# Attention transposes in runs over two PSUM banks held as one tile

## The chip, the cores and the metric

The kernel runs on one core of a Trainium2 chip. The core has five engines that run side by side: TensorE (in the profile PE for its matmuls, PEld for the weight loads ahead of them), VectorE (DVE), ScalarE (ACT), GpSimd (POOL) and SyncE (SP), which issues most DMA transfers. Matmuls write to PSUM, which has eight banks of 128 partitions x 512 fp32 values; DVE and ACT read it from there. The metric is the time of one execution on the device in microseconds (us); lower is better.

## The reference

One residual block over 1040 positions (16 learned meta tokens and 1024 frames), model width 1024, in fp32:

```
xn   = rms_norm(h, g0);  proj = xn @ w_in
o_a  = forgetting_attention(q_a, k_a, v_a, log_f)     # 8 heads of 64: softmax(q k^T/8 + c[t] - c[s]), s <= t
o_b  = stick_breaking_attention(q_b, k_b, v_b)        # 8 heads of 64: sigmoid(z[t,s]) * prod_{s<j<t}(1 - sigmoid(z[t,j]))
mix  = (sigmoid(g_a)*(o_a @ w_o_fox) + sigmoid(g_b)*(o_b @ w_o_sb)) @ w_out
h    = h + rms_norm(mix, g1)
u    = causal_depthwise_conv(rms_norm(h, g2) @ w_up)  # 3 taps
h    = h + rms_norm((gelu(u_gate)*u_val) @ w_down, g3)
```

Only the attention of both kinds, and the projections that run beside it, bear on what follows.

## The kernel before

Every fp32 operand is split into a high and a low part, and a product is made of three matmuls: high x high, high x low, low x high (`products`, L118). Data lie with features on the partitions and positions along the row, in three pieces of 260, 390 and 390 positions (`PCS`).

The attention runs over 16 heads, first eight forgetting ones (b = 0), then eight stick-breaking ones (b = 1). `prep(x + 1)` projects queries and keys of the next head (`qk_head`, tile pq) and, for each second head, the values of a pair of heads (`v_pair`, tile pv), while `attention` works on the present one; after that `gate(x)` projects a block of the gates (tile pg). The last seven gates follow behind the heads.

`attention` takes the queries in four blocks c of 256, two times 128. `weights_of` makes the two tiles of attention weights (pr, with queries on the partitions): scores by matmuls into a bank of psS, then for a forgetting head exponential and normalization, for a stick-breaking head two sigmoids and a product scan along the row on DVE (L403). The weights must then have keys on the partitions, so TensorE transposes them, 128 x 128 at a time, into a bank of psT: first the 16 meta keys (tile tm, L414, two transposes), then for each g up to c a group of up to four (tile tr, L424; three where g = c, since one of the four is above the diagonal). ACT copies the bank to the high part of pt (L428), DVE subtracts that from the bank for the low part (L429), and matmuls of pt with the values add into the one bank of psO (tile po, L418 and L434). Per head that is 8 transposes into tm and 36 into tr. The values need transposes too: eight into two tiles vtr (L300) and one into vtm (L305) for each pair of heads.

The eight banks of PSUM in this part: two for projections (pool pl, tile tag lin); psS, psT and psO share six, 3 + 2 + 1 for forgetting and 2 + 3 + 1 for stick-breaking heads. A tile of a pool can be taken again when everything that reads the one before it in that bank has been done. Each engine runs its instructions in one fixed order. A planner makes that order when the program is built, with a model of the instructions' times; the order of the source is its priority. `after(ins)` lets an instruction be issued on its engine only behind `ins`. The hardware then runs each engine's list in order, and an instruction that waits holds up all behind it on that engine.

At the start the first values (pv) go through psT, and the norm's sums and row (`rstd_row`, L138 to L151, tiles rp and rr) through psS.

Of the kernel before, what the change touches and what calls it, by code (L numbers as in the profile page):

```python
# [8 lines left out]
F32 = mybir.dt.float32  # L9
F32R = mybir.dt.float32r  # L10
AF = mybir.ActivationFunctionType
ALU = mybir.AluOpType
# [4 lines left out]
P = 128  # L17
# [32 lines left out]
def block_kernel(ctx, tc, xa, xb, wqk, wv, wf, bfg, wg, wo, wout, wup, wdn, gains, conv, cst, out):  # L50
    nc = tc.nc

    def f(ap):
        return ap.bitcast(F32)
# [110 lines left out]
    with ExitStack() as pa:  # L165
# [4 lines left out]

        pps = pa.enter_context(ExitStack())

        def psum_pools(ns, nt):
            pps.close()
            return [pps.enter_context(tc.tile_pool(name=n, reuse_waits="tile", bufs=k, space=PSUM))
                    for n, k in (("psS", ns), ("psT", nt), ("psO", 1))]

        psS, psT, psO = psum_pools(3, 2)

        ap1 = pa.enter_context(tc.tile_pool(name="ap1", reuse_waits="tile", bufs=1))  # L180
        ap2 = pa.enter_context(tc.tile_pool(name="ap2", reuse_waits="tile", bufs=2))
# [23 lines left out]
        def x_stats(i):  # L205
            n0, n1 = PCS[i]
            w = n1 - n0
            ss = []
            for k in range(0, KT, 4):
                sq = n1p.tile([P, 4, w], F32, tag="sq", bufs=1, name=f"sq{i}{k}")  # L210
                xk = xrs[i][:, k : k + 4, :]
                if i == 0:
                    nc.scalar.activation(sq, xk, AF.Square)
                else:
                    nc.gpsimd.tensor_tensor(sq, xk, xk, op=ALU.mult)
                ss.append(n1p.tile([P, w], F32, tag="ss", name=f"ss{i}{k}"))
                nc.vector.tensor_reduce(ss[-1], sq.rearrange("p k t -> p t k"), axis=AX.X, op=ALU.add)
            nc.scalar.copy(rs1[:, n0:n1], rstd_row(ss, w, n1p, psS, "s", f"a{i}"))


        def forget():
# [59 lines left out]
        def v_pair(b, p):  # L281
            hi, lo = load_w(wv[b * 4 + p], KT * P, f"v{b}{p}", hv=b or p)
            yield
            vt = ap1.tile([P, L], F32, tag="vt", name=f"vt{b}{p}")
            for i, (n0, n1) in enumerate(PCS):
                if b == 0 and p == 0:
                    ps = psT.tile([P, 512], F32, tag="tr", name=f"pv{b}{p}{i}")
                else:
                    ps = pl.tile([P, 512], F32, tag="lin", name=f"pv{b}{p}{i}")
                products(ps[:, : n1 - n0], hi, lo, xs[i], 0, KT, 0, n1 - n0)  # L290
                with tc.high_priority(offset=200):
                    nc.vector.tensor_tensor(vt[:, n0:n1], ps[:, : n1 - n0], rs1[:, n0:n1], op=ALU.mult)
                yield
            vps, vtag = (psT, "tr") if b else (psS, "s")
            vv = ap2.tile([P, 8, 2, 2, DH], F32R, tag="vv", name=f"vv{b}{p}")
            for g in range(2):
                pt = vps.tile([P, 4, 2, DH], F32, tag=vtag, name=f"vtr{b}{p}{g}")
                for j in range(4):
                    c0 = NM + (4 * g + j) * P
                    nc.tensor.transpose(pt[:, j, :, :].rearrange("p a b -> p (a b)"), vt[:, c0 : c0 + P], ident)  # L300
                hv = vv[:, 4 * g : 4 * g + 4, :, 0, :]
                nc.scalar.copy(hv, pt)
                nc.vector.tensor_tensor(vv[:, 4 * g : 4 * g + 4, :, 1, :], pt, f(hv), op=ALU.subtract)
            pt = vps.tile([P, 4, 2, DH], F32, tag=vtag, name=f"vtm{b}{p}")
            nc.tensor.transpose(pt[0:NM, 0, :, :].rearrange("p a b -> p (a b)"), vt[:, 0:NM], ident)  # L305
            vm = vms[p % 2]
            src = pt[0:NM, 0, :, :]
            nc.scalar.copy(vm[0:NM, :, 0, :], src)
            nc.scalar.copy(vm[32:48, :, 0, :], src)
            nc.vector.tensor_tensor(vm[0:NM, :, 1, :], src, f(vm[0:NM, :, 0, :]), op=ALU.subtract)  # L310
            nc.vector.tensor_tensor(vm[32:48, :, 1, :], src, f(vm[0:NM, :, 0, :]), op=ALU.subtract)
            st = ap2.tile([NM, 2, DH], F32, tag="vst", bufs=1, name=f"vst{b}{p}")
            nc.scalar.copy(st, src)
            for hh in range(2):
                h = 2 * p + hh
                nc.sync.dma_start(vmini[b][NM * h : NM * (h + 1), :], st[:, hh, :])
            yield vv, vm
# [45 lines left out]
        def weights_of(b, h, qk, i):  # L363
# [40 lines left out]
                nc.gpsimd.tensor_tensor(pr[:, : w - 1], pr[:, : w - 1], kp[:, 1:w], op=ALU.mult)  # L404
            return pr

        def attention(b, h, qk, vv, vm):
            p, hh = h // 2, h % 2
            for c in range(4):
                prs = [weights_of(b, h, qk, 2 * c + tb) for tb in range(2)]  # L410
                po = psO.tile([P, 256], F32, tag="o", name=f"po{b}{h}{c}")
                tm = psT.tile([P, 512], F32, tag="tr", name=f"tm{b}{h}{c}")
                for tb in range(2):
                    nc.tensor.transpose(tm[0:NM, tb * P : (tb + 1) * P], prs[tb][:, 0:NM], ident)  # L414
                pm = ptm[c % 2]
                nc.scalar.copy(pm[0:NM, :], tm[0:NM, 0:256])
                nc.vector.tensor_tensor(pm[32:48, :], tm[0:NM, 0:256], f(pm[0:NM, :]), op=ALU.subtract)
                nc.tensor.matmul(po, vm[:, hh, :, :].rearrange("p a b -> p (a b)"), pm, start=True, stop=False)  # L418
                for g in range(c + 1):
                    last = g == c  # L420
                    tl = [(2 * g, 0), (2 * g, 1)] + ([] if last else [(2 * g + 1, 0)]) + [(2 * g + 1, 1)]
                    tr = psT.tile([P, 512], F32, tag="tr", name=f"tr{b}{h}{c}{g}")
                    for x, (j, tb) in enumerate(tl):
                        nc.tensor.transpose(tr[:, x * P : (x + 1) * P],  # L424
                                            prs[tb][:, NM + j * P : NM + (j + 1) * P], ident)
                    n = P * len(tl)
                    pt = apl.tile([P, 2, 512], F32R, tag="pt", bufs=3, name=f"pt{b}{h}{c}{g}")
                    nc.scalar.copy(pt[:, 0, :n], tr[:, :n])  # L428
                    nc.vector.tensor_tensor(pt[:, 1, :n], tr[:, :n], f(pt[:, 0, :n]), op=ALU.subtract)  # L429
                    for j in range(2):  # L430
                        vj = vv[:, 2 * g + j, hh, :, :].rearrange("p a b -> p (a b)")
                        for s in range(2):
                            o0 = P if (last and j == 1) else 0
                            nc.tensor.matmul(po[:, o0:256], vj, pt[:, s, 256 * j : min(256 * j + 256, n)],  # L434
                                             start=False, stop=(last and j == 1 and s == 1))
                ot = apl.tile([DH, 256], F32, tag="ot", name=f"ot{b}{h}{c}")
                nc.scalar.copy(ot, po[DH:P, :])
                os_ = apl.tile([DH, 256], F32, tag="os", name=f"os{b}{h}{c}")
                nc.vector.tensor_tensor(os_, po[0:DH, :], ot, op=ALU.add)
                nc.sync.dma_start(od[b][p][hh * DH : (hh + 1) * DH, 2 + 256 * c : 258 + 256 * c], os_)  # L440
                if c == 0 and h == NH - 1:
                    mini(b)

        def mini(b):
# [12 lines left out]
            else:  # L457
                nc.scalar.activation(w, s, AF.Sigmoid)
                nc.scalar.activation(s, s, AF.Sigmoid, scale=-1.0)
                for h in range(NH):  # L460
                    r = s[:, h, :][:, ::-1]
                    nc.vector.tensor_tensor_scan(r, r, r, 1.0, op0=ALU.mult, op1=ALU.bypass)
                nc.vector.tensor_tensor(w[:, :, 0 : NM - 1], w[:, :, 0 : NM - 1], s[:, :, 1:NM], op=ALU.mult)
            tp = psT.tile([P, 512], F32, tag="tr", name=f"mt{b}")
            nc.tensor.transpose(tp[:, 0:2], w.rearrange("p a b -> p (a b)"), ident[0:2, 0:2])
            e = ap1.tile([P, 2], F32, name=f"me{b}")
            nc.scalar.copy(e, tp[:, 0:2])
            x = ap1.tile([P, NH, 2], F32, name=f"mx{b}")
            nc.vector.tensor_tensor(x, e.unsqueeze(1).to_broadcast([P, NH, 2]),
                                    bmask.unsqueeze(2).to_broadcast([P, NH, 2]), op=ALU.mult)  # L470
            po = psT.tile([P, 512], F32, tag="tr", name=f"mo{b}")
            nc.tensor.matmul(po[0:DH, 0:16], vmini[b], x.rearrange("p a b -> p (a b)"), start=True, stop=True)
            o = ap1.tile([DH, NH, 2], F32, name=f"mos{b}")
            nc.scalar.copy(o, po[0:DH, 0:16].rearrange("p (a b) -> p a b", a=NH))
# [48 lines left out]
        for x, (b, h) in enumerate(heads):  # L523
            qk, (vv, vm) = nxt
            attention(b, h, qk, vv, vm)
            if x + 1 == NH:
                psS, psT, psO = psum_pools(2, 3)
                kpp = side_pool("kpp", 2)
                smask = kpp.tile([P, 2, P], F32R, tag="mask", bufs=1, name="smask")
                raw = apl.tile([P, L], F32, tag="pr", bufs=6, name="smask_raw")[:, :P]  # L530
                nc.sync.dma_start(raw, cst[:, CW + P : CW + 2 * P])
                nc.vector.tensor_copy(smask[:, 0, :], ident)
                nc.vector.tensor_copy(smask[:, 1, :], raw)
            if x + 1 < len(heads):
                nxt = prep(x + 1)
            if x < len(heads) - LATE:
                gate(x)
# [552 lines left out]
```

## Time and profile before

| | |
|---|---|
| median of 3 runs | 1690.51 us (1689.75 to 1694.01) |
| profiled execution | 1691.7 us, span of its instructions 1689.8 us |
| granted TensorE clock, mean | 0.992 of full speed |
| TensorE matmul busy | 1644.3 us, 97% of the span |
| DVE, ACT, POOL busy | 1098.2, 819.9, 450.4 us |
| attention's transposes (tr) | first at 103.3 us, last at 729.9 us |

A row of a group reads: line, engine, operation, tiles written <- read, shape, count | busy time in all, mean duration in ns | idle time of the engine just before, and who ended it. The recorded durations of matmuls overlap: the next one starts well before the end of the one before, so what one costs is read from the distance between starts. A row of the timeline merges neighbouring instructions of one kind: start, length from the first start to the last end, count.

### The profile page before, as it was taken

To read this page: it belongs to the slowest core of one execution; us is meant where nothing else is said; L and a number is where in the kernel's file an instruction comes from. 1 tells how busy PE (TensorE), PEld (TensorE's weight loads), DVE (VectorE), ACT (ScalarE), POOL (GpSimd) and SP (SyncE) were. 2 spreads that over 40 slices of the span, in tenths; PEclk is the share of its full clock that TensorE was granted. 3 is DMA by queue.
4 is the path that set the end of the run, shared out by engine and by line. 5 is a ranking of instruction groups with operands and counts; after the bars stand their busy time and mean duration, and the time that the engine had idled before them with its cause. 6 is when DMAs were issued, how large, how long until landed. Compare 5 with 4: busy or idle time off the path is not lost.

```text
span 1689.8 us, 29746 instructions
## 1 busy us (share of the span) xinstructions
PE 1644.3 (97%) x11656; PEld 1584.0 (94%) x11656; DVE 1098.2 (65%) x1849; ACT 819.9 (49%) x1702; POOL 450.4 (27%) x312
## 2 busy tenths in 40 slices
PE   6999999999999999999999999999999999999997
PEld 6899999999999999999999999999999999787787
DVE  8555656655677776745535887888987867333622
ACT  4334545534566665543434555556555556333321
POOL 3446566655566665412211000000000000000001
PEclk9899999999999999999999999999999999999999
DMA  4122121221211111255343452333322226344741
GB/s 170 54 66 65 50 68 57 59 70 49 64 42 28 45 42 50 68 176 176 120 128 111 144 194 91 99 116 121 107 85 91 93 89 213 123 148 138 239 125 63
DMA packets 78076, 170.59 MB, mean 101 GB/s; under 512 B 10320, under 2 KB 33616, under 8 KB 77936
## 3 DMA queue, kind: packets, MB, share of 16 engines
q1 hardware_dynamic: 77392, 168.16, 31.4%
q8 instruction: 92, 1.51, 0.4%
q10 hardware_dynamic: 544, 0.52, 0.1%
q14 instruction: 48, 0.39, 0.1%
HBM read 126.43 MB, written 35.77 MB: 96 GB/s over the span
## 4 chain that ended last, share of the span: by engine, by line
PE 86%; DVE 5%; DMA 3%; issue 3%; ACT 2%; POOL 0%; SPq 0%; DVEq 0%; ACTq 0%; POOLq 0%
PE A L799 12%; PE pd L928 11%; PE pq L118 10%; PE pg L118 9%; PE B L799 6%; PE pm L622 6%; PE y L118 5%; PE pv L118 4%; PE pu L622 4%; PE po L434 4%; PE tr L424 4%; PE R L799 3%; PE s L352 2%; PE s L353 2%; DMA gr<-gdr 2%
## 5 line engine op out<-in xcount | busy, mean ns | idle before, releaser
L974 POOL TENSOR_TENSOR acc<-acc,hr 128x512 f32<-128x512 f32 x4 | 5.0, 1276 | 737.0 <-DVE acc L967 737.0
L928 PE MATMUL pd<-g,wh_d 128*128 128x512 f32 x616 | 193.3, 394 | 2.9 <-ACT wh_d L106 1.6
L928 PEld LDWEIGHTS pd<-g,wh_d 128*128 128x128 f32 x616 | 115.4, 188 | 30.8 <-ACT wh_d L106 2.8
L729 DVE SCALAR_TENSOR_TENSOR c<-us,cb,c 128x512 f32<-128x512 f32 x176 | 128.6, 745 | 23.1 <-ACT c L727 22.4
L400 POOL TENSOR_SCALAR pr<-pr,mx 128x144 f32<-128x144 f32 (+3 forms) x64 | 114.7, 1797 | 102.9 <-DVE mx L399 67.5
L429 DVE TENSOR_TENSOR pt<-tr,pt 128x512 fp32r<-128x512 f32 (+1 forms) x160 | 98.5, 632 | 49.2 <-ACT pt L428 46.2
L928 PE MATMUL pd<-g,wl_d 128*128 128x512 f32 x308 | 121.2, 394 | 2.0 <-DVE wl_d L92 1.9
L403 DVE TENSOR_TENSOR_SCAN kp<-kp 128x144 f32<-128x144 f32 (+3 forms) x64 | 101.9, 1605 | 23.1 <-ACT kp L385 21.3
L434 PE MATMUL po<-pt,vv 128*128 128x256 f32 (+1 forms) x640 | 110.1, 280 | 1.3 <-DVE pt L429 1.2
L404 POOL TENSOR_TENSOR pr<-pr,kp 128x143 f32<-128x143 f32 (+3 forms) x64 | 82.6, 1300 | 97.8 <-DVE kp L403 61.5
L92 DVE TENSOR_TENSOR wl_d<-wr_d,wh_d 128x896 fp32r<-128x896 f32 (+1 forms) x42 | 47.7, 1136 | 92.4 <-ACT wh_d L106 91.1
L428 ACT CAST pt<-tr 128x512 fp32r<-128x512 f32 (+1 forms) x160 | 83.3, 545 | 42.4 <-PE tr L424 40.6
L393 ACT ACTIVATE pr<-s,mx 128x144 f32<-128x144 f32 (+6 forms) x112 | 59.8, 540 | 76.2 <-DVE mx L391 60.5
L434 PEld LDWEIGHTS po<-pt,vv 128*128 128x128 f32 x640 | 94.5, 189 | 2.2 <-DVE pt L429 1.6
L424 PE MATMUL tr<-cs,pr 128*128 128x128 f32 x576 | 91.5, 274 | 0.0
L106 ACT CAST wh_d<-wr_d 128x896 fp32r<-128x896 f32 (+1 forms) x42 | 41.1, 979 | 97.0 <-PE pd L928 84.3
L352 PE MATMUL s<-k,q 128*128 128x264 f32 (+9 forms) x240 | 80.4, 338 | 0.2
L118 PE MATMUL pq<-xh,wh_qk 128*128 128x390 f32 (+1 forms) x384 | 79.1, 331 | 0.0
L727 ACT ACTIVATE c<-us,cb 128x512 f32<-128x512 f32 x88 | 71.7, 816 | 14.2 <-DMA gdr<-c 9.2
L118 PE MATMUL pq<-xl,wh_qk 128*128 128x390 f32 (+1 forms) x384 | 78.5, 331 | 0.0
L118 PE MATMUL pq<-xh,wl_qk 128*128 128x390 f32 (+1 forms) x384 | 77.8, 328 | 0.0
L118 PE MATMUL pg<-xh,wh_g 128*128 128x390 f32 (+1 forms) x384 | 73.9, 324 | 2.0 <-DVE qkt L333 1.5
(291 smaller groups left out, 4550.8 us busy)
## 6 DMA issues: line engine op xcount, KB each, us to landing
wu<-in_wup SPq DMA_DIRECT2D x40, 512.0 KB, 3.3
wr_d<-in_wdn SPq DMA_DIRECT2D x28, 448.0 KB, 3.6
gdr<-c SPq DMA_DIRECT2D x44, 256.0 KB, 2.5
gr<-gdr SPq DMA_DIRECT2D x44, 256.0 KB, 4.0
gs<-gd SPq DMA_DIRECT2D x16, 513.0 KB, 5.0
wr_qk<-in_wqk SPq DMA_DIRECT2D x16, 512.0 KB, 3.8
wr_g<-in_wg SPq DMA_DIRECT2D x16, 512.0 KB, 3.2
wr_wo<-in_wout SPq DMA_DIRECT2D x16, 512.0 KB, 3.4
```

The costliest lines, as they stand in the source:

```text
L118: marks["mm"] = nc.tensor.matmul(ps, w[:, k * P : (k + 1) * P], x[:, k - k0, n0:n1], start=(k == k0 and s == 0), stop=(k == k1 - 1 and s = ...
L352: nc.tensor.matmul(ps[:tn, :n], q2[:, t0 : t0 + tn], k1[:, s0:s1], start=True, stop=False)
L400: nc.gpsimd.tensor_scalar(pr[:, :w], pr[:, :w], z, None, op0=ALU.mult)
L403: nc.vector.tensor_tensor_scan(r, r, r, 1.0, op0=ALU.mult, op1=ALU.bypass)
L424: nc.tensor.transpose(tr[:, x * P : (x + 1) * P], prs[tb][:, NM + j * P : NM + (j + 1) * P], ident)
L428: nc.scalar.copy(pt[:, 0, :n], tr[:, :n])
L429: nc.vector.tensor_tensor(pt[:, 1, :n], tr[:, :n], f(pt[:, 0, :n]), op=ALU.subtract)
L434: nc.tensor.matmul(po[:, o0:256], vj, pt[:, s, 256 * j : min(256 * j + 256, n)], start=False, stop=(last and j == 1 and s == 1))
L622: nc.tensor.matmul(ps, (hi, hi, lo)[s][:, c : c + P], xs[kh][s == 1][:, k, :], start=(s == 0 and kh == 0 and k == 0), stop=(s == 2 and kh ...
L729: nc.vector.scalar_tensor_tensor(c, u[:, :, tap : tap + 256], cb[:, x, tap : tap + 1], c, op0=ALU.mult, op1=ALU.add)
L799: nc.tensor.matmul(ps, w[:, (k0 + i) * P : (k0 + i + 1) * P], x[:, i, :], start=(first and s == 0 and i == 0), stop=(s == 2 and i == 3), s ...
L928: nc.tensor.matmul(ps, a[:, (k - k0) * P : (k - k0 + 1) * P], x[:, c0:c1], start=(k == 0 and s == 0), stop=(k == NK - 1 and s == 2))
```

## The change

The two (or three) single banks of psT become one tile of two banks (tag tr), taken and given back as a whole; in the stick-breaking heads a third bank (tag one) takes what needs only one. `banks` hands these out. A new function `turned` makes one run: for a block c, the groups of keys are taken as [0] together with the meta keys, then [1, 2], then [3]. All transposes of a run are written first, in reversed order, the one whose input is made last in front, and the rest issued behind it; after that come the copies, subtractions and products of the run's groups. A forgetting head so has 1 + 2 + 2 + 3 = 8 runs. The values' two tiles vtr are one run too, each transpose behind the one in front of it, for forgetting heads now also in psT instead of psS. At the start the first values go to psS instead of psT, and the norm's sums and row to the one bank of psO instead of psS. Counted over the program, 137 places remain at which TensorE changes from a transpose to a product, instead of 214.

```diff
-        def psum_pools(ns, nt):
+        def psum_pools(ns):
             pps.close()
             return [pps.enter_context(tc.tile_pool(name=n, reuse_waits="tile", bufs=k, space=PSUM))
-                    for n, k in (("psS", ns), ("psT", nt), ("psO", 1))]
+                    for n, k in (("psS", ns), ("psT", 1), ("psO", 1))]
-        psS, psT, psO = psum_pools(3, 2)
+        psS, psT, psO = psum_pools(3)
+        def banks(b, n, name):
+            if n == 1 and b:
+                return [psT.tile([P, 512], F32, tag="one", name=name)]
+            two = psT.tile([P, 2, 512], F32, tag="tr", name=name)
+            return [two[:, i, :] for i in range(n)]
...
-            nc.scalar.copy(rs1[:, n0:n1], rstd_row(ss, w, n1p, psS, "s", f"a{i}"))
+            nc.scalar.copy(rs1[:, n0:n1], rstd_row(ss, w, n1p, psO, "o", f"a{i}"))
...
-                    ps = psT.tile([P, 512], F32, tag="tr", name=f"pv{b}{p}{i}")
+                    ps = psS.tile([P, 512], F32, tag="s", name=f"pv{b}{p}{i}")
...
-            vps, vtag = (psT, "tr") if b else (psS, "s")
-            for g in range(2):
-                pt = vps.tile([P, 4, 2, DH], F32, tag=vtag, name=f"vtr{b}{p}{g}")
+            lead = None
+            vts = [t.rearrange("p (j a b) -> p j a b", j=4, a=2) for t in banks(b, 2, f"vtr{b}{p}")]
+            for g, pt in enumerate(vts):
                 for j in range(4):
                     c0 = NM + (4 * g + j) * P
-                    nc.tensor.transpose(pt[:, j, :, :].rearrange("p a b -> p (a b)"), vt[:, c0 : c0 + P], ident)
+                    with after(lead):
+                        lead = nc.tensor.transpose(pt[:, j, :, :].rearrange("p a b -> p (a b)"), vt[:, c0 : c0 + P], ident)
+            for g, pt in enumerate(vts):
                 hv = vv[:, 4 * g : 4 * g + 4, :, 0, :]
...
+        def turned(b, h, c, gs, prs, po, vv, vm):
+            hh = h % 2
+            jobs = []
+            free = banks(b, len(gs) + (gs[0] == 0), f"tr{b}{h}{c}{gs[0]}")
+            if gs[0] == 0:
+                tm = free.pop(0)
+                jobs.append((tm, [(tm[0:NM, tb * P : (tb + 1) * P], prs[tb][:, 0:NM]) for tb in (1, 0)]))
+            tls = {}
+            for g in gs:
+                last = g == c
+                tls[g] = [(2 * g, 0), (2 * g, 1)] + ([] if last else [(2 * g + 1, 0)]) + [(2 * g + 1, 1)]
+                tr = free.pop(0)
+                jobs.append((tr, [(tr[:, x * P : (x + 1) * P], prs[tb][:, NM + j * P : NM + (j + 1) * P])
+                                  for x, (j, tb) in reversed(list(enumerate(tls[g])))]))
+            lead = None
+            for _, turns in reversed(jobs):
+                for dst, src in turns:
+                    with after(lead):
+                        t = nc.tensor.transpose(dst, src, ident)
+                    lead = lead or t
...
+            for g, (tr, turns) in zip(gs, jobs):
+                pt = apl.tile([P, 2, 512], F32R, tag="pt", bufs=3, name=f"pt{b}{h}{c}{g}")
+                nc.scalar.copy(pt[:, 0, :n], tr[:, :n])
+                nc.vector.tensor_tensor(pt[:, 1, :n], tr[:, :n], f(pt[:, 0, :n]), op=ALU.subtract)
...
+                for gs in [[0]] + [list(range(g, min(g + 2, c + 1))) for g in range(1, c + 1, 2)]:
+                    turned(b, h, c, gs, prs, po, vv, vm)
```

More of the change, by code (lines that the diff above doesn't have):

```diff
@@ L303, in v_pair @@
                 nc.vector.tensor_tensor(vv[:, 4 * g : 4 * g + 4, :, 1, :], pt, f(hv), op=ALU.subtract)
-            pt = vps.tile([P, 4, 2, DH], F32, tag=vtag, name=f"vtm{b}{p}")
+            pt = banks(b, 1, f"vtm{b}{p}")[0].rearrange("p (j a b) -> p j a b", j=4, a=2)
             nc.tensor.transpose(pt[0:NM, 0, :, :].rearrange("p a b -> p (a b)"), vt[:, 0:NM], ident)
@@ L405, in weights_of @@
             return pr
+        def turned(b, h, c, gs, prs, po, vv, vm):
[18 more added lines that the diff above has]
+                    lead = lead or t
+            if gs[0] == 0:
+                tm = jobs.pop(0)[0]
+                pm = ptm[c % 2]
+                nc.scalar.copy(pm[0:NM, :], tm[0:NM, 0:256])
+                nc.vector.tensor_tensor(pm[32:48, :], tm[0:NM, 0:256], f(pm[0:NM, :]), op=ALU.subtract)
+                nc.tensor.matmul(po, vm[:, hh, :, :].rearrange("p a b -> p (a b)"), pm, start=True, stop=False)
+            for g, (tr, turns) in zip(gs, jobs):
+                last = g == c
+                n = P * len(turns)
+                pt = apl.tile([P, 2, 512], F32R, tag="pt", bufs=3, name=f"pt{b}{h}{c}{g}")
+                nc.scalar.copy(pt[:, 0, :n], tr[:, :n])
+                nc.vector.tensor_tensor(pt[:, 1, :n], tr[:, :n], f(pt[:, 0, :n]), op=ALU.subtract)
+                for j in range(2):
+                    vj = vv[:, 2 * g + j, hh, :, :].rearrange("p a b -> p (a b)")
+                    for s in range(2):
+                        o0 = P if (last and j == 1) else 0
+                        nc.tensor.matmul(po[:, o0:256], vj, pt[:, s, 256 * j : min(256 * j + 256, n)],
+                                         start=False, stop=(last and j == 1 and s == 1))
         def attention(b, h, qk, vv, vm):
@@ L411, in attention @@
                 po = psO.tile([P, 256], F32, tag="o", name=f"po{b}{h}{c}")
[L412 to L435, printed above, removed]
+                for gs in [[0]] + [list(range(g, min(g + 2, c + 1))) for g in range(1, c + 1, 2)]:
+                    turned(b, h, c, gs, prs, po, vv, vm)
                 ot = apl.tile([DH, 256], F32, tag="ot", name=f"ot{b}{h}{c}")
@@ L463, in mini @@
                 nc.vector.tensor_tensor(w[:, :, 0 : NM - 1], w[:, :, 0 : NM - 1], s[:, :, 1:NM], op=ALU.mult)
-            tp = psT.tile([P, 512], F32, tag="tr", name=f"mt{b}")
+            tp = banks(b, 1, f"mt{b}")[0]
             nc.tensor.transpose(tp[:, 0:2], w.rearrange("p a b -> p (a b)"), ident[0:2, 0:2])
@@ L470, in mini @@
                                     bmask.unsqueeze(2).to_broadcast([P, NH, 2]), op=ALU.mult)
-            po = psT.tile([P, 512], F32, tag="tr", name=f"mo{b}")
+            po = banks(b, 1, f"mo{b}")[0]
             nc.tensor.matmul(po[0:DH, 0:16], vmini[b], x.rearrange("p a b -> p (a b)"), start=True, stop=True)
@@ L526, in block_kernel @@
             if x + 1 == NH:
-                psS, psT, psO = psum_pools(2, 3)
+                psS, psT, psO = psum_pools(2)
                 kpp = side_pool("kpp", 2)
```

## The prediction

> **What bounds the kernel now.** I read the page first, then the windows by stage, then the groups of TensorE, then single stretches of the timeline.
>
> ```profile
> PE 1644.3 (97%) x11656; PEld 1584.0 (94%) x11656; DVE 1098.2 (65%) x1849; ACT 819.9 (49%) x1702; POOL 450.4 (27%) x312
> ...
> PE 86%; DVE 5%; DMA 3%; issue 3%; ACT 2%; POOL 0%; SPq 0%; DVEq 0%; ACTq 0%; POOLq 0%
> ```
>
> TensorE is busy for 97% of the span, and 86% of the chain that ended last lies on it. A change to the transposes can therefore pay only in two ways: less TensorE time per instruction, or less waiting. The windows show how much waiting there is.
>
> ```profile
> 17.00:60.00 43.00, 39.25 (x205) 37.64 (x205) 33.89 (x33) 8.64 (x18) 20.80 (x10) 0.80 0.24 88
> ...
> 103.00:390.00 287.00, 287.00 (x2000) 284.13 (x1999) 174.34 (x469) 137.46 (x384) 174.24 (x110) 1.00 0.21 61
> ...
> 420.00:735.00 315.00, 307.69 (x2182) 301.84 (x2182) 225.57 (x310) 183.48 (x469) 177.72 (x123) 0.99 0.17 49
> ```
>
> The columns are length, then busy time of PE, PEld, DVE, ACT and POOL, then granted clock. In the forgetting heads (103 to 390 us) PE is never idle: nothing can be gained from a wait there, only lost. In the stick-breaking heads (420 to 735 us) it is idle for 315.0 - 307.7 = 7.3 us. At the start (17 to 60 us) it is idle for 3.8 us and its clock is 0.80. Behind 735 us the change touches nothing.
>
> **Instructions.** The change neither adds nor removes an instruction on an engine; it moves them.
>
> ```profile
> L424 PE MATMUL tr<-cs,pr 128*128 128x128 f32 x576 | 91.5, 274 | 0.0
> ...
> L414 PE MATMUL tm<-cs,pr 128*16 128x128 f32 x128 | 28.9, 272 | 0.0
> ...
> L300 PE MATMUL vtr<-cs,vt 128*128 128x128 f32 x64 | 9.7, 275 | 0.7 <-DVE vt L292 0.7
> ...
> L305 PE MATMUL vtm<-cs,vt 128*16 128x128 f32 x8 | 2.2, 272 | 0.0
> ```
>
> That is 576 + 128 + 64 + 8 = 776 transposes before and after, and the same products. The last column matters: the attention's transposes, 704 of them, have never held PE up (0.0 us of idle time before them).
>
> **What a change from transpose to product costs.** The words of the change count 214 such places before and 137 after, 77 fewer. Their price can be read where short runs of transposes stand among equal products:
>
> ```profile
> 403.50 0.49 PE L424 MATMUL tr<-cs,pr 128*128 128x128 f32 x3
> 403.75 0.49 PE L118 MATMUL pq<-xl,wh_qk 128*128 128x260 f32 x2
> 404.08 0.51 PE L434 MATMUL po<-pt,vv 128*128 128x256 f32 x3
> 404.43 0.38 PE L414 MATMUL tm<-cs,pr 128*16 128x128 f32 x2
> 404.56 0.48 PE L118 MATMUL pq<-xl,wh_qk 128*128 128x260 f32 x2
> 404.88 1.12 PE L118 MATMUL pq<-xh,wl_qk 128*128 128x260 f32 x8
> 405.84 0.34 PE L118 MATMUL pq<-xh,wh_qk 128*128 128x390 f32 x1
> ```
>
> Eight undisturbed products take 405.84 - 404.88 = 0.96 us, 0.12 each. The two products behind a run of transposes take 0.33 us (403.75 to 404.08) and 0.32 us (404.56 to 404.88) where 0.24 would do: each change seems to cost some 0.08 us. But the run ahead of them is short by as much. Inside a run one transpose takes (0.49 - 0.27) / 2 = 0.11 us, its recorded duration being 0.27; three of them would be 0.33 us, and the product starts after 0.25; two would be 0.22, and it starts after 0.13. So the last transpose of a run occupies PE for about 0.03 us and the product behind it for 0.08 more, and the two add up to what a transpose inside a run costs. Over both places: 3 transposes and 2 products took 0.58 us against 0.33 + 0.24 = 0.57; 2 and 2 took 0.45 against 0.46. The price of a change is 0.00 us, give or take 0.01. I take 3 ns: 77 x 3 ns = **0.2 us gained**. The upper bound, if only the 0.08 us behind the run counted, is 77 x 0.083 = 6.4 us; it speaks against it that the first row is short by the same time, so I take the near end.
>
> **What the two-bank tile costs.** Before, each of two banks (three in the stick-breaking heads) comes free by itself. Afterwards the next run waits until both banks are read: transposes, copy by ACT, subtraction by DVE, and the second bank's subtraction behind the first one's. This pair of tiles shows the time:
>
> ```profile
> 306.67 0.60 PE L424 MATMUL tr<-cs,pr 128*128 128x128 f32 x4
> 307.03 0.40 PE L352 MATMUL s<-k,q 128*128 128x328 f32 x1
> ...
> 311.21 0.64 PE L434 MATMUL po<-pt,vv 128*128 128x256 f32 x4
> 311.68 0.60 PE L424 MATMUL tr<-cs,pr 128*128 128x128 f32 x4
> ```
>
> ```profile
> 307.24 0.68 DVE L429 TENSOR_TENSOR pt<-tr,pt 128x512 fp32r<-128x512 f32 x1
> 307.84 0.83 DVE L383 TENSOR_REDUCE mx<-s 128x1 f32<-128x264 f32 x2
> 308.58 0.68 DVE L429 TENSOR_TENSOR pt<-tr,pt 128x512 fp32r<-128x512 f32 x1
> ```
>
> ```profile
> L428 ACT CAST pt<-tr x160: 452/578/644, 105.4 to 730.2; 128x512 fp32r<-128x512 f32 x96, 128x384 fp32r<-128x384 f32 x64
> L429 DVE TENSOR_TENSOR pt<-tr,pt x160: 526/679/693, 106.1 to 730.7; 128x512 fp32r<-128x512 f32 x96, 128x384 fp32r<-128x384 f32 x64
> L424 PE MATMUL tr<-cs,pr x576: 270/272/301, 103.3 to 729.9; 128*128 128x128 f32 x192
> ```
>
> From the last start of a run: 0.27 + 0.58 + 0.68 + 0.68 = 2.2 us until both banks are read, and the pair above did it in 309.26 - 307.03 = 2.2 us. The room for it: 16 heads in 729.9 - 103.3 us are 39.2 us each. A forgetting head has eight runs (one, two, two and three for its four blocks of queries) and, per pair of heads, two for the values, nine in all: one every 4.35 us. Here PE had 311.68 - 307.03 = 4.65 us of other work between two transposes. A full run of eight is 8 x 0.11 = 0.9 us; 0.9 + 2.2 = 3.1 us of 4.35. On average the wait is hidden by the products that stand between the runs, and I cost it at **nothing in the forgetting heads**. If this cover is gone, it costs up to 2.2 us a run: the transpose that waits holds up everything behind it on PE (pq, pg, po, scores), and DVE's drains of those wait in turn.
>
> In the stick-breaking heads the same subtractions queue behind the scans:
>
> ```profile
> L403 DVE TENSOR_TENSOR_SCAN kp<-kp 128x912 f32<-128x912 f32 x8 | 21.6, 2701 | 2.6 <-ACT kp L385 2.6
> L403 DVE TENSOR_TENSOR_SCAN kp<-kp 128x1040 f32<-128x1040 f32 x8 | 20.1, 2514 | 6.3 <-ACT kp L385 5.3 <-POOL kb L92 1.0
> ...
> L403 DVE TENSOR_TENSOR_SCAN kp<-kp 128x784 f32<-128x784 f32 x8 | 14.3, 1786 | 0.4 <-ACT kp L385 0.3
> ```
>
> There single-bank runs have a bank of their own, so the pair is taken six times a head, but I keep the tighter 4.35 us, since runs are not evenly spread. A scan of up to 4.35 - 2.2 = 2.1 us in front of a subtraction stays hidden; the 784 wide ones do, the 912 and 1040 wide ones exceed it by 0.6 and 0.4 us. If each of these 16 met an evacuation: 8 x 0.6 + 8 x 0.4 = 8 us; if none, 0. I take a third, since scans are 101.9 us of these 315, **2.7 us lost**.
>
> **The other edits.** At the start the sums of the norm move to the one bank of the output pool, the first values from the two transposed banks to the three score banks.
>
> ```profile
> 35.65 1.69 PE L118 MATMUL pv<-xh,wh_v 128*128 128x390 f32 x8 [1.45 <-DVE vt L292]
> ...
> 38.91 1.72 PE L138 MATMUL rp_a<-cs,ss 128*128 128x1 f32 x14 [0.85 <-DVE ss L217]
> ...
> 51.39 2.95 PE L138 MATMUL rp_a<-cs,ss 128*128 128x1 f32 x14 [1.45 <-DVE ss L217]
> ```
>
> The 1.45 us at 35.65 may go, as a third bank is free; but the sums behind wait for DVE anyway, at 38.91 and again at 51.39, and DVE would be late next. One bank for the sums costs nothing for the same reason: each set waits for DVE's reduction, not for a bank. I take 0; the ends are -1.45 us and, from the clock of 0.80 over 43 us (8.6 us lost, which another pattern of waits could halve or raise by half), about 4 us either way. The first transpose of a run is now the one whose input is ready last; those that ran ahead of it before leave early by less, which moves no work. No DMA is added, and none is moved past another in program order.
>
> **Sum.** Profiled execution 1691.7 us (span 1689.8 and 1.9 around it) - 0.2 + 0 + 2.7 + 0 = 1694.2. It lies 1.2 us above the median of 1690.51 shown, so a median of **1693 us**.
>
> **Rivals.**
> *B, the pair's wait shows: slower.* In 4 places of each forgetting head and 2 of each stick-breaking one, a run follows another of the same block of queries, with its input long there: 8 x 4 + 8 x 2 = 48 places. The tile alone decides when it may start. If the written order keeps there only the 8 products of the run in front (8 x 0.12 = 1 us), 2.2 - 1.0 = 1.2 us is lost each time; it decides as soon as less than 2.2 us of other work stands between two runs. All 48 would be 58 us; I price one in four, 12 x 1.2 = 14 us: 1705 us. For it: banks go from two or three that turn to one pair, and the forgetting heads have no idle time to absorb anything. Against it: 4.65 us stood between above. The Trainium skill's Perfetto Trace Analysis (Optimizing Tensor Performance, Matmuls) speaks against this change: independent groups should rotate through different banks, so that the evacuation of one lies under the matmuls of the next. No row of before shows a transpose that lacked a bank, so it is not yet borne out here.
> *C, faster.* Either the 0.08 us behind a run is real after all, -6.4 us, or the re-planned order loses most of the 7.3 us of idle time in the stick-breaking heads: 1684 us either way. Against the first stand the rows at 403.50 and 404.43; for the second, that all instructions there are placed anew; against it:
>
> ```profile
> PE pv L118 <- DVE qkt L333: 3.2, 2, 1.9
> ```
>
> these waits are for drains behind scans, which the change leaves alone.
> *D, it doesn't do what it says.* Each transpose is tied only to the first of its run, so products could still be placed inside: 1691 us.
>
> **Chances.** A (1693, own range 1688 to 1698) 0.39; B 0.33; C 0.25; D 0.03. About 0.3%, 5 us, is what can be told from no change. A: 0.31 same, 0.03 faster, 0.05 slower; B: 0.30 slower, 0.03 same; C: 0.22 faster, 0.03 same; D same. Faster 0.25, same 0.40, slower 0.35. The range reaches down over C with the clock's 4 us, to 1680, and up over B to one and a half times its price, to 1713.
>
> **What would show it.** Right: the same 776 transposes at 0.11 us inside a run, products behind a run still 0.08 us late, idle time before the transposes under 3 us, PE full from 103 to 390 us. B: idle time before transposes, released by DVE's subtraction. C: the sum of transpose and product falling below its parts, or the stick-breaking window idle for under 2 us. What I take on trust is that the order keeps work between the runs; a changed clock at the start would also make me wrong.

## The result

The changed kernel takes 1835.3 us (median of 4 runs, 1832.7 to 1837.7) where the kernel before takes 1690.2 us: ratio 1.085, 95% interval 1.083 to 1.088. It is slower by 145 us, far outside the range of 1680 to 1713 us.

The page of the changed kernel, parts 1 and 4, with the granted clock of part 2:

```profile
PE 1712.7 (93%) x11656; PEld 1623.2 (88%) x11656; DVE 1104.2 (60%) x1849; ACT 828.6 (45%) x1702; POOL 446.1 (24%) x312
...
PEclk9999898989989989999699999999999999999998
...
PE 76%; DVE 9%; ACT 5%; DMA 4%; issue 4%; POOL 1%; SPq 0%; DVEq 0%; ACTq 0%; POOLq 0%
```

The instructions are the same in number (11656 matmuls), but TensorE's share of the chain fell from 86 to 76%, DVE's and ACT's rose, and the clock is below full in slices where it was full before.

For the stages, cut at the first transpose of the first head, that of the ninth head (the first stick-breaking one) and the first product of the output projections (tile y), here are the windows of the kernel before, and then of the changed one. Columns: length, busy PE, PEld, DVE, ACT, POOL, clock, share and rate of the DMA.

```profile
103.20:456.50 353.30, 352.30 (x2443) 348.34 (x2441) 215.03 (x560) 169.34 (x468) 208.19 (x135) 1.00 0.20 60
456.50:751.10 294.60, 288.30 (x2044) 283.10 (x2043) 210.65 (x289) 172.02 (x435) 160.96 (x109) 0.99 0.20 56
```

```profile
103.70:523.80 420.10, 391.31 (x2443) 371.60 (x2442) 216.92 (x558) 172.51 (x469) 206.38 (x136) 0.93 0.17 50
523.80:885.70 361.90, 319.71 (x2084) 302.05 (x2082) 210.52 (x278) 171.34 (x420) 156.51 (x108) 0.95 0.16 46
885.70:998.50 112.80, 99.78 (x769) 97.73 (x770) 60.00 (x133) 48.02 (x86) 25.16 (x31) 0.92 0.47 142
```

The forgetting heads lost 66.8 us, the stick-breaking heads 67.3; of the difference of the spans, 146.1 us, 12 are left for all else, most of it the first products of y. Of the 66.8 us, idle time of PE is 28.8 - 1.0 = 27.8; the other 39.0 us are in PE's busy time, which grew with the same 2443 matmuls. The clock of 0.93 accounts for some 0.07 x 420 = 29 us of that.

The loss is not spread over the heads. For the first pair of heads:

```profile
103.70:179.60 75.90, 75.75 (x518) 74.97 (x517) 41.92 (x118) 34.07 (x96) 47.60 (x31) 1.00 0.23 69
179.60:209.00 29.40, 22.64 (x96) 18.91 (x96) 13.77 (x39) 11.00 (x29) 8.52 (x6) 0.71 0.02 5
```

For 76 us PE is full at full clock; then come 29 us with 96 matmuls, 6.8 us of idle time and a clock of 0.71. The other three pairs go the same way: PE almost full for 74 to 75 us, then 29.3, 28.9 and 33.4 us at a clock of 0.77, 0.76 and 0.74. Nearly all idle time of these heads, and every fall of the clock, lies in these four dry stretches at the end of each pair.

What PE waited for in the changed kernel, the longest first in total:

```profile
PE po L453 <- DVE pt L448: 15.9, 27, 1.6
PE rp_a L138 <- DVE ss L224: 14.5, 3, 10.9
PE y L118 <- DVE t L616: 11.9, 1, 11.9
PE po L442 <- DVE ptm L441: 9.8, 9, 1.7
PE s L361 <- ACT pr L395: 6.6, 11, 1.9
PE po L453 <- ACT pt L447: 6.0, 13, 0.7
...
PE vtm L314 <- DVE mx L400: 4.4, 2, 2.3
...
PE vtm L314 <- DVE vv L312: 2.4, 1, 2.4
...
PE tr L435 <- POOL pr L413: 1.3, 1, 1.3
```

The attention's transposes (tr) still wait for almost nothing, 1.3 us. Most of the wait stands before the products po of a run, for the copy and the subtraction of their own run: 15.9 + 9.8 + 6.0 = 31.7 us, 12.4 of them in the forgetting heads. There the values' meta transposes (vtm) wait another 4.4 + 2.4 = 6.8 us, behind the reading of the values' pair of banks. When a transposed group has not yet been read, nothing else is left in PE's order to do.

Two stretches show how that comes. First a filled one, at the start of the heads: the runs on PE, and on DVE the subtraction that ends each run's hold of the pair (the time from its first transpose until both banks have been read).

```profile
103.66 0.71 PE L435 MATMUL tr<-cs,pr 128*128 128x128 f32 x5
...
111.08 0.82 PE L435 MATMUL tr<-cs,pr 128*128 128x128 f32 x6
...
118.50 0.49 PE L435 MATMUL tr<-cs,pr 128*128 128x128 f32 x3
...
122.77 0.81 PE L435 MATMUL tr<-cs,pr 128*128 128x128 f32 x6
```

```profile
106.09 0.56 DVE L448 TENSOR_TENSOR pt<-tr,pt 128x384 fp32r<-128x384 f32 x1 [0.55 <-ACT pt L447]
...
114.02 0.68 DVE L448 TENSOR_TENSOR pt<-tr,pt 128x512 fp32r<-128x512 f32 x1
...
119.54 0.56 DVE L448 TENSOR_TENSOR pt<-tr,pt 128x384 fp32r<-128x384 f32 x1 [1.78 <-ACT pt L447]
```

The pair was free at 106.65, 114.70 and 120.10 us; the next run came 4.4, 3.8 and 2.7 us later, 7.4, 7.4 and 4.3 us after the one in front. In between PE worked through projections and scores. Second, a dry stretch, 80 us later:

```profile
184.13 0.84 PE L435 MATMUL tr<-cs,pr 128*128 128x128 f32 x6
185.87 0.38 PE L442 MATMUL po<-ptm,vm 128*128 128x256 f32 x1 [0.90 <-DVE ptm L441]
186.49 0.38 PE L453 MATMUL po<-pt,vv 128*128 128x256 f32 x1 [0.23 <-ACT pt L447]
187.21 0.62 PE L453 MATMUL po<-pt,vv 128*128 128x256 f32 x3 [0.34 <-DVE pt L448]
187.67 1.82 PE L435 MATMUL tr<-cs,pr 128*128 128x128 f32 x8
190.22 3.08 PE L453 MATMUL po<-pt,vv 128*128 128x256 f32 x8 [0.73 <-ACT pt L447]
193.10 0.84 PE L435 MATMUL tr<-cs,pr 128*128 128x128 f32 x3
```

Not one projection stands between these runs. PE goes from transposes to waiting to the run's own products and on, and the clock falls to half: eight transposes take 1.82 us here.

Why there is no projection to fill in: PE had done two of the three pieces of the next pair's values (pv) by 178.7 us, and the third comes only at 202.42.

```profile
178.16 0.70 PE L118 MATMUL pv<-xh,wl_v 128*128 128x390 f32 x3
...
196.86 1.61 PE L308 MATMUL vtr<-cs,vt 128*128 128x128 f32 x8
...
201.53 0.37 PE L314 MATMUL vtm<-cs,vt 128*16 128x128 f32 x1 [2.33 <-DVE mx L400]
202.42 2.97 PE L118 MATMUL pv<-xh,wh_v 128*128 128x390 f32 x8 [0.52 <-DVE vt L299]
```

```profile
201.94 0.90 DVE L299 TENSOR_TENSOR vt<-pv,rs 128x260 f32<-128x260 f32 x2 [0.49 <-PE vtm L314]
```

The two pieces fill both projection banks. DVE can drain them into vt only when the present pair's values have been transposed out of vt, and those transposes now go through the same pair of banks, behind the attention's runs: at 196.86 and 201.53 us. So from 178.7 to 202.4 us no projection of any kind starts, though the third piece and the next heads' queries and keys are still to be done. The other pairs of the forgetting heads stop at the same place, and so do the stick-breaking heads (no projection from 582.9 to 606.7 and from 673.6 to 698.7 us). In the kernel before, the last of these transposes starts at 172.56 us for the first pair, and the next pv at 172.84. Where it has the same stop, it is shorter: 448.9 to 452.2 us, and 514.5 to 522.7 in the stick-breaking heads.

The hold itself is also longer than two banks by themselves would make it. The run of eight at 187.67 is read so, with nothing else on ACT or DVE:

```profile
189.58 0.58 ACT L447 CAST pt<-tr 128x512 fp32r<-128x512 f32 x1 [3.14 <-PE tr L435]
190.92 0.59 ACT L447 CAST pt<-tr 128x512 fp32r<-128x512 f32 x1 [0.76 <-DVE pt L448]
```

```profile
190.20 0.69 DVE L448 TENSOR_TENSOR pt<-tr,pt 128x512 fp32r<-128x512 f32 x1 [3.04 <-ACT pt L447]
191.54 0.69 DVE L448 TENSOR_TENSOR pt<-tr,pt 128x512 fp32r<-128x512 f32 x1 [0.66 <-ACT pt L447]
```

ACT copies the second bank only when DVE has subtracted from the first, so the two engines take turns; both banks are read at 192.23 us, 4.56 us after the first transpose. In the whole kernel ACT waited so for DVE's reading of the other bank 53 times, 40.4 us in all:

```profile
ACT pt L447 <- DVE ptm L441: 23.5, 31, 2.3
...
ACT pt L447 <- DVE pt L448: 11.6, 17, 1.3
...
ACT vv L311 <- DVE vv L312: 5.3, 5, 1.3
```

The kernel before, and the run single below, in which the same runs go to single banks, list no such wait.

### The profile page after: what moved, and what is told of

It reads as the page before. It is cut to its first block, busy times and chain, and to the rows that moved or that the text cites. A ratio compares the mean times of both kernels' runs of the same rounds, so it can differ in the third digit from the quotient of the medians.

```text
span 1835.9 us, 29628 instructions
## 1 busy us (share of the span) xinstructions
PE 1712.7 (93%) x11656; PEld 1623.2 (88%) x11656; DVE 1104.2 (60%) x1849; ACT 828.6 (45%) x1702; POOL 446.1 (24%) x312
## 3 DMA queue, kind: packets, MB, share of 16 engines
q1 hardware_dynamic: 77392, 168.16, 28.9%
## 4 chain that ended last, share of the span: by engine, by line
PE 76%; DVE 9%; ACT 5%; DMA 4%; issue 4%; POOL 1%; SPq 0%; DVEq 0%; ACTq 0%; POOLq 0%
PE pd L955 11%; PE A L826 9%; PE pq L118 9%; PE pg L118 9%; PE pm L649 5%; PE y L118 5%; PE pu L649 5%; PE B L826 5%; PE tr L435 4%; PE po L453 3%; PE pv L118 3%; PE R L826 2%; PE s L361 2%; PE s L362 1%; DVE pt L448 1%
## 5 line engine op out<-in xcount | busy, mean ns | idle before, releaser
L955 PE MATMUL pd<-g,wh_d 128*128 128x512 f32 x616 | 194.9, 398 | 4.1 <-ACT wh_d L106 3.1
L453 PE MATMUL po<-pt,vv 128*128 128x256 f32 (+1 forms) x640 | 133.8, 306 | 23.3 <-DVE pt L448 15.9
L453 PEld LDWEIGHTS po<-pt,vv 128*128 128x128 f32 x640 | 105.5, 203 | 39.0 <-DVE pt L448 26.1
L412 DVE TENSOR_TENSOR_SCAN kp<-kp 128x144 f32<-128x144 f32 (+3 forms) x64 | 109.5, 1722 | 23.9 <-ACT kp L394 20.5
L435 PE MATMUL tr<-cs,pr 128*128 128x128 f32 (+1 forms) x704 | 104.3, 286 | 1.3 <-POOL pr L413 1.3
L361 PE MATMUL s<-k,q 128*128 128x264 f32 (+9 forms) x240 | 85.0, 356 | 11.2 <-ACT pr L395 6.6
L118 PE MATMUL y<-o,wh_o 128*128 128x258 f32 x512 | 77.8, 294 | 17.7 <-DVE t L616 11.9
L118 PEld LDWEIGHTS y<-o,wh_o 128*128 128x128 f32 x512 | 70.0, 199 | 19.9 <-DVE t L616 12.1
L395 ACT ACTIVATE pr<-s 128x144 f32<-128x144 f32 (+6 forms) x112 | 49.3, 453 | 73.4 <-PE tr L435 73.2
L435 PEld LDWEIGHTS tr<-cs,pr 128*128 128x128 f32 (+1 forms) x704 | 78.4, 137 | 3.1 <-POOL pr L413 1.5
```

Source lines behind the costliest of these rows:

```text
L118: marks["mm"] = nc.tensor.matmul(ps, w[:, k * P : (k + 1) * P], x[:, k - k0, n0:n1], start=(k == k0 and s == 0), stop=(k == k1 - 1 and s = ...
L361: nc.tensor.matmul(ps[:tn, :n], q2[:, t0 : t0 + tn], k1[:, s0:s1], start=True, stop=False)
L435: t = nc.tensor.transpose(dst, src, ident)
L955: nc.tensor.matmul(ps, a[:, (k - k0) * P : (k - k0 + 1) * P], x[:, c0:c1], start=(k == 0 and s == 0), stop=(k == NK - 1 and s == 2))
```

## The experiments

Theory **H**: the pair, held as one, sets the pace. Rival **V**: the values' transposes of the forgetting heads, now in the same ring of banks behind the attention's runs, keep their buffer and the two projection banks taken. Rival **P**: the tie inside a run holds TensorE up. The first four runs:

```diff
# v_back: the forgetting heads' values in the score banks again
-vts = [... banks(b, 2, f"vtr{b}{p}")]
+vts = [... (banks(b, 2, f"vtr{b}{p}") if b else [psS.tile(..., tag="s") for g in range(2)])]
# (vtm likewise)
# single: banks given back one by one, psT of 2 and 3 banks
-two = psT.tile([P, 2, 512], F32, tag="tr", name=name)
-return [two[:, i, :] for i in range(n)]
+return [psT.tile([P, 512], F32, tag="tr", name=f"{name}_{i}") for i in range(n)]
# no_pin
-with after(lead):
+with after(None):
# before_v_moved, on the kernel before
-vps, vtag = (psT, "tr") if b else (psS, "s")
+vps, vtag = psT, "tr"
```

> The changed kernel, but the values' tiles vtr and vtm of the forgetting heads stand in the score banks again. Theory H (the pair held as one sets the pace: 9 holds in a forgetting head took 52.5 us, so one is some 5.8 us): 8 holds a head instead of 9, 8 x 5.8 = 47 us less, 1788 us, and the stick-breaking heads unchanged at 357 us. Theory V (the values' run stands behind the attention's runs in one ring, so their buffer and both projection banks stay taken): the whole loss of the forgetting heads, 420 - 353 = 67 us, goes, 1768 us. Theory P (the order inside a run, each behind the first, holds TensorE up): 1835 us.

> The changed kernel, but the banks of a run are single tiles again, two for forgetting and three for stick-breaking heads, each given back by itself; runs, their order and the values' place stay as changed. H: back to the kernel before, 1690 us, give or take 10. V: the forgetting heads keep their 67 us, the others lose them not: 1757 us. P: 1835 us.

> The changed kernel without the tie of each of a run's transposes to the first. H and V: 1835 us, within 5. P: under 1800 us.

> The kernel before with one edit: the values' tiles of the forgetting heads stand in the transposes' two single banks instead of the score banks. H: 1690 us, within 10. V: 1757 us. P: 1690 us.

Measured, one run each beside the kernel before at 1693: v_back 1804.6 us, single 1710.7, no_pin 1832.4, before_v_moved 1693.2. **P falls**: without the tie nothing changes, and the order has as many changes from transpose to product as with it (139, counted in both traces; the kernel before has 216). **H holds** in the main: with banks given back one by one, in the same runs, 124.6 of the 145 us are gone. V as the cause of the whole loss falls, since it forecast 1757 for single and for before_v_moved, and 1768 for v_back. What single takes away is both the joint giving back and the turns that ACT and DVE take; no run parts these two. Yet H put the ninth hold of a head at 5.8 us and the run gave 24.7 us over eight heads, 3.1 us each. The windows of v_back and single, stages cut as above:

```profile
101.80:497.20 395.40, 374.78 (x2443) 361.01 (x2442) 214.59 (x558) 172.61 (x469) 206.40 (x136) 0.96 0.18 53
497.20:858.60 361.40, 320.52 (x2085) 302.82 (x2083) 210.65 (x279) 171.48 (x420) 156.65 (x108) 0.95 0.15 46
```

```profile
102.90:474.90 372.00, 362.57 (x2439) 353.63 (x2438) 213.56 (x557) 168.76 (x469) 206.64 (x135) 0.98 0.19 57
474.90:770.00 295.10, 288.23 (x2039) 282.51 (x2038) 205.36 (x282) 168.39 (x428) 160.74 (x108) 0.99 0.18 53
```

With single banks the stick-breaking heads are back at 295 us; the forgetting heads keep 372 - 353 = 19 us. Moving the values back helps less than V said. One reason may be that the stop remains: in v_back the forgetting heads' values are still transposed late (at 261.86 us for the second pair, with no projection from 255 to 264 us), though no longer in the pair.

The next question: does the chip need so long a hold, or is it the written order? The filled stretch points to the second. Theory **H1**: the planner takes the hold to be about 6 us, fills it with projections until they run out, and leaves the later runs bare. Theory **H2**: the chip can go no faster. To tell them apart, the projections beside a head's eight runs were tied, eight matmuls at a time, in turn behind these runs:

```diff
# paced, on the changed kernel (the same for the values and the gates)
+led.setdefault(NH * b + h, []).append(t)          # the last transpose of each run, in turned()
+turnsq = paced(y, of(y)[0], 9 + sum(of(y)))       # y = the head whose runs stand beside it
-products(ps[:, :w], hi, lo, xs[i], 0, KT, 0, w)
+products(ps[:, :w], hi, lo, xs[i], 0, KT, 0, w, [next(turnsq) for _ in range(3)])
# no_low and before_no_low: the low part left out
-nc.vector.tensor_tensor(pt[:, 1, :n], tr[:, :n], f(pt[:, 0, :n]), op=ALU.subtract)
-nc.tensor.matmul(po[:, o0:256], vj, pt[:, s, 256 * j : ...], ...)
+nc.tensor.matmul(po[:, o0:256], vj, pt[:, 0, 256 * j : ...], ...)
# single_v_back: the edits of single and of v_back together
```

> The changed kernel with the same tile, runs and arithmetic, but the projections that stand beside a head's eight runs are tied, eight matmuls at a time, in turn behind these runs, so that none can be used up early. Theory H1 (the planner takes the pair's hold for some 6 us and fills it with projections until they run out; the chip needs some 3 us, so where projections are left nothing waits): the gaps close, 1835 falls to 1700 to 1740 us, and the clock in the forgetting heads goes back to 1.00. Theory H2 (the chip itself can't go faster than the pair's hold): no change, 1820 to 1840 us.

> The changed kernel without the subtractions of the attention weights' low part (the products use the high part twice): the computation of that low part is left out. A hold then ends with ACT's copy of the second bank, on the chip about 1.4 us sooner. H1 and H2: the pace rises with the shorter hold; 128 runs x 1.4 us or more is 180 us, more than all that was lost, so TensorE becomes the bound again: 1690 to 1720 us. If the hold did not set the pace, DVE's relief alone would count, as in the next run, which takes the same from the kernel before.

> The same left out of the kernel before (low part of the attention weights not computed). All theories: TensorE stays the bound, 1680 to 1690 us.

> Single banks as in the run before of that kind, and the forgetting heads' values in the score banks again: what is left of the change is the grouping into runs and the start's two moves. H: as the kernel before, 1690 us, within 5. If the runs' grouping itself costs (a group must wait for the weights of both tiles of queries): 1700 to 1711 us. If fewer changes from transpose to product paid 0.08 us each: 1684 us.

Measured: paced 1757.6 us (ratio to before 1.039, 1.036 to 1.043), no_low 1754.5, before_no_low 1686.0, single_v_back 1695.6 (ratio 1.003, 1.002 to 1.004). Tying instructions down, which can only restrict the planner, took 78 us off, with the tile, the runs and the number of changes (137 in the trace) as they were: H2 falls. H1 is not shown by it in full: the ties also put all pieces of the next pair's values behind the transposes of the present ones (in the first pair 193.6 us behind 190.8), so the stop at the full projection banks is gone along with the early use, and the trace of the changed kernel has projections blocked, not run out. The time did not come down to the 1700 to 1740 us of H1; the clock in the forgetting heads came back to 0.97, not 1.00. Leaving out the subtractions shortened the changed kernel by 81 us and the kernel before by about 5, which fits a kernel that pays for the length of the hold; without the subtractions ACT's second copy also has less of DVE's to wait for. The forecast of 1690 to 1720 was too far: the stops remain, the first from 182.2 to 194.9 us. And single_v_back, runs kept but neither the joint hold nor the values' move, is 5 us slower than before: grouping by itself gains nothing. It also shows the values' place as a second cost: its forgetting heads take 354.6 us where those of single take 372.0. The same move costs 25 us with the pair (420.1 against 395.4) and nothing on the kernel before (1693.2 us against 1693.1).

Then the parts were put together, and the even pace was tried on the faster kernel:

```diff
# paced_v_back: paced and v_back.  paced_single: paced, single and v_back.
# before_paced, on the kernel before: ties behind the ten groups tr of a head
+led.setdefault(NH * b + h, []).append(marks["t"])
+return iter([runs[min(j * 10 // n, 9)] for j in range(first, n)] + ...)
# before_v1, on the kernel before
-vps, vtag = (psT, "tr") if b else (psS, "s")
+vps, vtag = psS, "s"
```

> The changed kernel with the projections tied in turn behind a head's runs, and the forgetting heads' values in the score banks again: 8 holds a head, at the even pace. H1 (early use of the projections and the ninth hold are what cost in the forgetting heads): these heads, 381.5 us when only paced, come to 353 to 362 us, and the whole to 1730 to 1740 us, the stick-breaking heads keeping their 335 us. H2 (the chip's own hold is the floor there): 375 us or more, 1750 us.

> Single banks given back one by one, runs, values in the score banks, and the projections tied in turn behind the runs. If early use of the projections is what costs only where the hold is long: 1690 to 1697 us, as without the ties (1695.6). If even spacing also spares the waits of the stick-breaking heads (7 us idle before): 1685 us.

> The kernel before with the projections tied in turn behind the ten groups of transposes of a head. Same question on the faster of the two kernels: 1683 to 1688 us if even spacing spares waits behind scans in the stick-breaking heads, 1690 to 1697 us if the planner's own order was already as good.

> The kernel before with one edit: in the stick-breaking heads too the values' tiles stand in the score banks (two there), not in the transposes' three. If the values' place behind the attention's transposes holds up projections there as it did with the pair: part of the 7.3 us of idle time between 420 and 735 us goes, 1684 to 1688 us. If those waits are for DVE behind its scans alone: 1690 us, within 2; if two score banks are too few for scores and values, 1692 to 1700 us.

Measured: paced_v_back 1734.1 us, paced_single 1712.4 (ratio 1.013, 1.011 to 1.016), before_paced 1706.8 (1.010, 1.009 to 1.012), before_v1 1701.8 (1.006, 1.004 to 1.009). The windows of paced_v_back, and then of paced_single:

```profile
97.60:457.80 360.20, 355.31 (x2442) 351.68 (x2441) 215.64 (x558) 174.05 (x470) 210.43 (x136) 0.99 0.20 58
457.80:793.00 335.20, 315.28 (x2159) 308.18 (x2159) 198.92 (x283) 173.35 (x420) 162.31 (x108) 0.97 0.16 47
```

```profile
99.10:453.20 354.10, 353.09 (x2438) 349.11 (x2438) 213.64 (x555) 167.08 (x465) 207.26 (x135) 1.00 0.19 58
453.20:773.60 320.40, 301.05 (x2114) 295.59 (x2115) 218.88 (x305) 181.81 (x455) 158.24 (x110) 0.98 0.22 65
```

In the forgetting heads the pair, evenly spaced and held eight times a head, costs 360.2 - 354.1 = 6 us, where without the ties it costs 395.4 - 354.6 = 41 (v_back against single_v_back): H1's 353 to 362. In the stick-breaking heads the rigid ties themselves cost some 24 us (320.4 with single banks against 296.1 in single_v_back), and the pair 15 more. Moving the values to the score banks there too, on the kernel before, made it slower, not faster.

Two more runs asked what those 15 us are, and whether the even pace is worth something in the forgetting heads alone:

```diff
# paced_v_back_no_low: paced_v_back and no_low
# before_paced_fox: before_paced with
+runs = led.get(y) if y < NH else None
```

> The changed kernel with tied projections and the values in the score banks, as before, and the subtractions of the attention weights' low part left out (it is not computed; the products use the high part twice). If in the stick-breaking heads the rest of the loss is the pair's wait for subtractions queued behind scans: these heads, 335.2 us with the subtractions, come to 320 us, what they take tied with single banks; the whole 1715 us or less. If the rest is the ties or the scans themselves: 330 us or more, 1727 us or more.

> The kernel before with the projections tied in turn behind the groups of transposes in the forgetting heads alone. Tied everywhere, their stage ended at 449.7 us instead of 456.5, and the stick-breaking heads took 24.5 us more. If the even pace is worth something where TensorE is the bound: 1690 - 7 = 1683 us. If the gain of the one stage is given back in the next: 1690 us, within 3.

Measured: paced_v_back_no_low 1713.4 us, its stick-breaking heads 453.9 to 772.6 us, 318.7 against 335.2 with the subtractions. That fits subtractions queued behind scans, but the same was not left out of paced_single, so a part may be DVE's relief alone. before_paced_fox 1690.5 us (ratio 1.000, 0.999 to 1.001): the earlier end of the forgetting heads (449.4 us instead of 456.5) is given back later. No version tried beats the kernel before; before_no_low, which leaves work out, is no rival to it.

## Why the prediction was wrong

**What held.** The price of a change from transpose to product. In the changed kernel, a run of seven and the products behind it:

```profile
235.56 0.93 PE L435 MATMUL tr<-cs,pr 128*128 128x128 f32 x7
236.25 0.61 PE L118 MATMUL pg<-xh,wh_g 128*128 128x390 f32 x2
236.69 1.58 PE L118 MATMUL pg<-xl,wh_g 128*128 128x390 f32 x8
238.11 1.60 PE L118 MATMUL pg<-xh,wl_g 128*128 128x390 f32 x8
```

Eight products take 238.11 - 236.69 = 1.42 us, 0.178 each. The seven transposes and two products took 236.69 - 235.56 = 1.13 us, and 7 x 0.11 + 2 x 0.178 = 1.13. The two products are 0.08 us late, the run 0.08 short, as predicted. The other kernels fit: with 243, 216, 196 and 135 changes in their traces (before_paced, before, single_v_back, paced_v_back), the forgetting heads took 351.3, 353.3, 354.6 and 360.2 us. They differ in more than the changes, but fewer changes never went with shorter heads. The rest of the list holds too: the same transposes, and no effect of the start's moves beyond a microsecond (first transpose of a head at 103.7 us against 103.2).

**The step that failed** is "On average the wait is hidden by the products that stand between the runs, and I cost it at nothing in the forgetting heads". It cost 66.8 us there, by two errors.

The average was the larger one. A run every 4.35 us was taken as if products would stand behind every run. In the first pair of heads each of the first twelve runs had 20 to 38 projection matmuls behind it, and PE lost nothing; the last four had none. The prediction counted the values' transposes as one more hold, and named what a waiting transpose holds up only for the case that the cover is gone. It did not see that these transposes take the cover away themselves: the drain of both projection banks waits for them, and with it every projection. With projections kept between the runs the pair costs 6 us in these heads (paced_v_back), so there the cover was enough.

The hold was too small as well. It was put at 2.2 us from the last transpose's start, 3.1 for a full run, with the second copy beside the first subtraction. A run of eight held the pair for 4.56 us at 187.67, at half clock, and for 4.57 us in a filled stretch at full clock (144.48 to 149.05), with other work of DVE in between. The first three holds above, 3.0, 3.6 and 1.6 us, are of shorter runs. The row that was to confirm the 2.2 us could not: the subtraction at 307.24 reads a bank whose transposes began at 305.72, nearly 1 us ahead of the row shown, and that bank was read by itself. That the two figures agreed was luck.

Why the planner put the values' transposes behind the last runs, and what it took the hold to be, stands in no trace. The 5.8 us of H is the mean of full and dry stretches, no length of a hold: in v_back eight holds went with 49.4 us a head, 6.2 each.

**The clock.** No term of the sum had it in the heads. In the forgetting heads about 29 of the 67 us are the clock's. From 180 to 198 us no wait was longer than 0.9 us, and the clock was halved from 187.8 on.

**Rival B** had the sign, but its place and its price were wrong. It put the wait before the transposes ("idle time before transposes"). Before the attention's there is 1.3 us; as it described it, the wait shows only before the values' meta transposes, 6.8 us; most stands before the products. Its 14 us, at most 58, counted one wait at a time, and neither the projections that stop nor the lost clock. The Trainium skill's rule named there, in Perfetto Trace Analysis (Optimizing Tensor Performance, Matmuls), that independent groups should rotate through banks, is borne out: the same runs with banks given back singly take 1710.7 us instead of 1835.3. The chance of 0.35 for slower was too low for a change whose direct gain had been found to be nothing.

**Second stage.** "2.7 us lost" stands against 67.3. Scans in front of the subtractions are suspects only for a smaller part, 15 us once the projections are spread, and even that is not parted from the longer hold. For the rest the trace shows the same stops as in the forgetting heads, 24 and 25 us long where the kernel before has 8 and 9; how much of the 67.3 us they make was not measured.

**Rivals C and D.** Nothing of C was seen: no sum fell below its parts, and idle time grew in both stages. D didn't occur: the trace has 139 changes where 137 were told, as the kernel before has 216 where 214 were.

## What to carry to other kernels

Before you merge buffers, ask for each thing that shares them what else stops while it waits. Here the values' transposes shared the pair; behind them waited the drain of both projection banks, and so all the work that was to cover the wait. An average of work per use can't show that; the written order can. Ask also whether the readers of the merged tile still work side by side, or take turns as ACT and DVE did here. And before you save a stall that shows behind an instruction, check whether the instruction ahead of it is short by the same time.

## What was not expected of the hardware

The granted clock fell to half in a stretch without any long wait. Two windows of the changed kernel, just before the fall and behind it:

```profile
184.30:187.70 3.40, 1.93 (x12) 1.22 (x11) 1.84 (x5) 1.31 (x3) 0.72 (x1) 1.00 0.08 19
187.80:198.00 10.20, 8.64 (x34) 7.09 (x33) 3.65 (x9) 3.94 (x11) 1.27 (x1) 0.50 0.00 0
```

Ahead of the fall PE was recorded busy for 1.93 of 3.4 us, with 12 matmuls and no wait longer than 0.9 us; the clock was then 0.50 for 10.2 us, though PE was recorded busy for 8.64 of them. The 34 matmuls in that window are no measure of what halved the clock, since at half the clock each takes longer (eight transposes 1.82 us at 187.67, 1.04 at 144.48). How little work is too little was not measured; other falls, as at 201.4 us, came behind a wait of 2.3 us. The Trainium skill's TensorE: Matmul & The Clock Gate (A second HAM failure mode: psum-queue depth-cycling) describes a kernel in which short idle times between groups of matmuls let the clock oscillate; this trace agrees.
